# Three blocks of one model on one core: a mixer's tables and loads placed anew, and a written order from a mixer's end to the last mlp

## The chip, the core and the metric

The kernel runs on one core of one Trainium2 chip. A core has a matmul engine (TensorE, here PE, whose weight loads are shown apart as PEld), three elementwise engines (VectorE or DVE, ScalarE or ACT, GpSimd or POOL) and SyncE (SP), whose queue issues most loads. Each runs its own list of instructions in order and waits on semaphores where it needs what another has made. SBUF is the working memory of 128 partitions; matmuls write into PSUM, in banks of 128x512 f32 here. PE's granted clock is 2.4 or 1.2 GHz, shown as 1.0 or 0.5 of full speed.

The metric is the device time of one execution in microseconds (us). Before the change it is the median of three runs, 2019.61 us.

## The reference

For 512 positions of width 1024, in float32. One layer has a state-space mixer, the next an index-selected attention, each followed by a gated mlp; then a block of a hybrid attention with four kinds of heads, cross attention into 256 memory rows and an mlp; a norm ends it. The parts that the change touches:

```python
def s5_mixer(u, lam_re, lam_im, log_dt, b_re, b_im, c_re, c_im, d_skip, w_glu):
    lam = lax.complex(lam_re.astype(f32), lam_im.astype(f32))     # 64 groups x 64 states
    dt = jnp.exp(log_dt.astype(f32))[:, None]
    a_bar = jnp.exp(lam * dt)
    b_bar = ((a_bar - 1.0) / lam)[..., None] * lax.complex(b_re.astype(f32), b_im.astype(f32))
    bu = jnp.einsum('blgh,gph->blgp', ug, b_bar)
    _, states = lax.associative_scan(_ssm_combine, (a_seq, bu), axis=1)   # s_t = a_bar s_(t-1) + bu_t
    y = jnp.einsum('blgp,ghp->blgh', states, c).real.reshape(bsz, length, D_MODEL)
    y = jax.nn.gelu(y + d_skip.astype(f32) * u.astype(f32))
    val, gate = jnp.split(y @ w_glu, 2, axis=-1)
    return val * jax.nn.sigmoid(gate)

def second_block(...):
    x = x + hybrid_mixer(rmsnorm_2(x, g_mix[l]), w_in[l], g_group[l], sinks[l], w_out[l], rel_table)
    x = x + memory_cross_attention(rmsnorm_2(x, g_cross[l]), rmsnorm_2(mem, g_mem[l]),
                                   w_xq[l], w_xkv[l], w_xo[l])
    x = x + squared_relu_mlp(rmsnorm_2(x, g_mlp[l]), w_up[l], w_down[l])
    return rmsnorm_2(x, g_final)
```

## The kernel before

The stream x lies feature-major in eight tiles `x[0..7]` of 128 features x 512 positions. For a matmul every float32 operand is split into a high and a low part (`xH`, `xL`; `wH` by ACT at L127, `wL` by DVE at L128), and `mm3` (L33 to L35) does three matmuls per product: high by high, low by high, high by low. A 128x1024 piece of weight is loaded, split, and used by 128x512 matmuls into a PSUM bank. Behind a block's last projection DVE adds a bank to `x[d]` (L295), ACT makes `xH`, DVE `xL` (L274), and the squares for the next norm are added up (ACT squares, POOL adds, DVE the last, L287). PE then sums them over partitions (`st`, L258), DVE takes the inverse root in small steps, and PE spreads the result over partitions (`bcps`, L247).

**The state-space mixer** (`s5`, 0 to about 150 us) works in chunks of eight positions, in four quarters q of 16 groups. At the start three small loads (`lam`) give the real and imaginary eigenvalues and `log_dt`; PE lays them out (`par`, L1247), DVE takes exponentials and angles (`dt`, `er`), POOL builds the tables of rotations (`rt`, `rsum`), DVE the powers `pw` and `bw`; meanwhile ACT squares the input and PE transposes the scaled input (`ups`). Each quarter then goes through:

- input tables: three products (L1400, 128x1024, a power from `bw` times `bt`) and two sums (L1406, L1407) of them; output tables alike from `pw` and `cv`. DVE makes all 24 products; POOL makes the sums, except the first two, which DVE makes;
- `rotation`: five operations on 128x512 for cosines and sines (L1442 to L1446), the first quarter's on DVE, the others on POOL;
- PE: transposes of the tables (`btps`), contributions of the chunks (`vps`, two banks), a small convolution kernel (`kps`, copied by 8 DMAs into a zeroed tile `toep`), the outputs (`yps`, 64 matmuls a quarter, from `toep` and the states `W`);
- DVE: the states, 14 operations on `vps` banks (L1510 to L1523), two scans among them.

`in_order` (L85) makes DVE, POOL, ACT and PE each keep the written order within the mixer; elsewhere a scheduler decides, from what it thinks each instruction costs. The written order of the quarters is the loop `for q in range(5)` at the function's end. PSUM banks go round in three groups by a tag: 4 banks of "pj", 2 of "sc", 2 of "tp".

**The end of the hybrid mixer** (1567 to 1610 us): the norm of the last head group is spread (`bcps<-ident,norm`), the group scaled and split, and the last part of the output projection (`w_out`, rows 768 to 1023, `lin`, 48 matmuls) added to x. Beside it PE has the values of the cross attention (`mv`, 48 matmuls). Then `queries` projects x for the cross attention (`w_xq`, 48 matmuls, also called `lin` there), with the norm's factor applied to the result; `st` and `bcps<-ident,rs_y` make that factor. **The cross attention** (1610 to 1646 us) makes scores (`xs`), exponentials (L1110) and outputs, projects them (`xo`) onto x, and the last mlp begins.

Of the kernel before, what the change touches and what calls it, by code (L numbers as in the profile page):

```python
# [9 lines left out]
F32 = mybir.dt.float32  # L10
F32R = mybir.dt.float32r
I32 = mybir.dt.int32
AF = mybir.ActivationFunctionType
# [3 lines left out]
P = 128  # L17
S = 512
D = 1024
KT = D // P  # L20
NB = S // P
# [54 lines left out]
def ps(k, name, tag="tp"):  # L76
    return k.psum.tile([P, 512], F32, tag=tag, name=name, bufs={"pj": 4, "sc": 2, "tp": 2}[tag])


def tmp(k, name="t", dt=F32):  # L80
    return k.tmp.tile([P, 512], dt, tag="tmp", name=name)


@contextmanager
def in_order(k, *engines):  # L85

    traced = k.nc.cur_bb.bb.instructions
    last = traced[-1]
    yield
    start = next(i for i in reversed(range(len(traced))) if traced[i] is last) + 1  # L90
    for e in engines:
        mine = [i for i in traced[start:] if i.engine == e.engine]
        for first, second in zip(mine, mine[1:]):
            k.tc.add_manual_dep(second, first.name, mybir.DependencyInfo(mybir.DependencyClass.NoSync,
                                                                         mybir.DependencyReason.DATA), reason="in order")


WK = 4
# [3 lines left out]
CROSS_RATIO = 2.0  # L102
# [48 lines left out]
def linear_fm(*args):  # L151
    run(linear_steps(*args))
# [100 lines left out]
def norm_finish(k, bcast=True, tag="tp"):  # L253

    nc = k.nc
    st = ps(k, "st", tag)
    for i in range(NB):
        nc.tensor.matmul(st[:, i:i + 1], k.acc[:, i * P:(i + 1) * P], k.ones, start=True, stop=True)  # L258
# [33 lines left out]
def update_late(k, d, b, gain, last):  # L292


    k.nc.vector.tensor_add(k.x[d], k.x[d], b)  # L295
    after_update(k, d, gain if d < last else None)
    if d == KT - 1:
        for e in range(last, KT):
            emit_hl(k, e, gain)


def set_apart(pool, n):
# [145 lines left out]
def drive(main, side, ratio):  # L448


    due = 0.0
    for t in main:
        due += t * ratio
        while due > 0:
            t = next(side, None)
            if not t:
                due = 0.0
            else:
                due -= t
    for _ in side:  # L460
        pass
# [308 lines left out]
def hybrid(k, next_gain):  # L770
    nc, a = k.nc, k.a
    w = a["w_in_2"][0]
    k.p_bufs = HYB_DEPTH + 1
    with ExitStack() as es:
# [104 lines left out]
        def apply_norm(g):  # L879
            rb = bcast_tokens(k, norms[g], None)  # L880
            for j in (2 * g, 2 * g + 1):
                nc.vector.scalar_tensor_tensor(y[j], y[j], gg[:, j:j + 1], rb, op0=ALU.mult, op1=ALU.mult)
                split_hl(k, k.xH[j], k.xL[j], y[j])
# [113 lines left out]
            yield from pipelined([head(g, h) for g in cols for h in range(4)], HYB_DEPTH)  # L997

        drive(main(), side(), HYB_RATIO)
        run(cr.values())  # L1000
        apply_norm(3)
        linear_fm(k, wo, 6 * P, k.xH[6:], k.xL[6:], 0, D, lambda d, b: update_late(k, d, b, "cross", 6))
        cr.queries()
        drive(cr.main(lambda d, b: update_late(k, d, b, next_gain, 6)), cr.heads(), CROSS_RATIO)


class Cross:
# [68 lines left out]
    def queries(self):  # L1076
        k = self.k
        self.q = []

        def ev(m, b):  # L1080
            u = tmp(k, "xq")
            k.nc.vector.tensor_mul(u, b, normed(k))
            self.q += stack_q(k, self.fr, u)

        linear_fm(k, k.a["w_xq_2"][0], 0, k.xH, k.xL, 0, 256, ev)

    def heads(self):
        k = self.k
# [99 lines left out]
def s5(k, x, next_gain):  # L1188
    nc, a = k.nc, k.a
    G2 = 32  # L1190
    with ExitStack() as es:
# [11 lines left out]

        lam = ep.tile([64, 3, 64], F32, name="lam")
        for i, n in enumerate(("s5_lambda_re", "s5_lambda_im")):
            nc.sync.dma_start(lam[:, i], a[n][0])
        nc.sync.dma_start(lam[:, 2, 0:1], a["s5_log_dt"][0][:, None])
        braw = []
        for n in ("s5_b_re", "s5_b_im"):
            t_ = ep.tile([G2, 2, 64, 16], F32, name=n)  # L1210
# [148 lines left out]
        def b_steps():  # L1359
# [11 lines left out]
            yield nc.vector.tensor_add(bt[2], bt[0], bt[1])  # L1371
            yield nc.vector.tensor_sub(bt[1], bt[1], bt[0])

        norm = []
        interleave((norm.append(y) or y for y in rsqrt_steps(k, sb[:, :8], 1.0 / D, 8, tag="s5n")), b_steps())
        rs = norm[0]
        xs = ep.tile([P, G2, 8, 16], F32, name="xs")
        for j in range(8):
            o, i_ = xs[:, :, 7 - j], xt[j].rearrange("p (g h) -> p g h", h=16)
            if j % 2:  # L1380
                nc.vector.tensor_scalar(o, i_, rs[:, j:j + 1], None, op0=ALU.mult)
            else:
                nc.scalar.activation(o, i_, AF.Copy, scale=rs[:, j:j + 1])

        U = []
        for g in range(8):
# [7 lines left out]
        def products(q, names, w, n0, v):  # L1394

            gs = slice(q * 8, q * 8 + 8)
            out = []
            for n, (wi, vi) in zip(names, ((2, 0), (0, 1), (1, 2))):
                t_ = (big(n, 2) if n[0] == "Q" else wide(n)).rearrange("p (a b c) -> p a b c", a=8, b=8)
                nc.vector.tensor_mul(t_, w[:, n0:n0 + 8, wi, gs].rearrange("p t g -> p g t")[:, :, :, None].to_broadcast(sh4),  # L1400
                                     v[vi][:, gs, None, :].to_broadcast(sh4))
# [10 lines left out]
        st_ = [Ctx() for _ in range(4)]  # L1412

        def mid(name, bufs, pool=None):
            return (pool or qp).tile([P, 8, 64], F32, tag=name, name=name, bufs=bufs)
# [32 lines left out]
        def chunk(q):  # L1448
            s = st_[q]
            B = s.B  # L1450

            BT = []
            for ri in range(2):
                t_ = wide(("raw", "wH")[ri]).rearrange("p (a b) -> p a b", a=8)
                for hh in range(2):
                    b = ps(k, "btps", "tp")
                    for i in range(4):
                        nc.tensor.transpose(b[:, i * P:(i + 1) * P], B[ri][:, hh * 4 + i].rearrange("p t h -> p (t h)"), k.ident)
                    nc.scalar.activation(t_[:, hh * 4:hh * 4 + 4].rearrange("p a b -> p (a b)"), b, AF.Copy)
                BT.append(t_)  # L1460
            s.V = []
            for ri in range(2):
                b = ps(k, "vps", "pj")
                for i in range(8):
                    for t in range(2):
                        nc.tensor.matmul(b[t * 64:(t + 1) * 64, i * 64:(i + 1) * 64], BT[ri][:, i, t * 64:(t + 1) * 64],
                                         U[2 * q + i // 4][:, i % 4, t], start=True, stop=True)
                s.V.append(b.rearrange("p (i c) -> p i c", c=64))

        def constants_of(q):  # L1470

# [126 lines left out]
        for q in range(5):  # L1598
            if q < 3:
                input_tables(q + 1)  # L1600
            if q < 4:
                st_[q].Q = sums(st_[q].Q, nc.gpsimd)
            if q < 3:
                rotation(q + 1, nc.gpsimd)
            if q:
                outputs(q - 1)
            if q < 3:
                constants_of(q + 1)
                chunk(q + 1)
# [131 lines left out]
```

## Time and profile before

| what | value |
|---|---|
| median of three runs | 2019.61 us (2014.90 to 2022.14) |
| profiled execution | 2023.27 us, its span 2021.5 us |
| PE busy | 1895.9 us (94%), mean clock 0.967 |
| PEld busy | 1575.7 us (78%) |
| DVE busy | 1139.8 us (56%) |
| ACT busy | 823.9 us (41%) |
| POOL busy | 452.0 us (22%) |

The busy times are sums over the whole span; what a stage is bound by is read from that stage. In lists of waits an idle time is put down to the releaser that came last. A timeline row gives the start, the busy time and the number of equal instructions it stands for; in brackets how long the engine was idle before and what ended that. SPq is SP's queue. A clock of 0.50 in a stretch is 1.2 GHz.

### The profile page before, as it was taken

The page shows a single profiled execution, that of the slowest core. Times are in us where ns is not written, and L with a number is a line of the kernel's source. Part 1 is how long each engine was busy: PE and PEld are TensorE (multiplying, and loading weights), DVE is VectorE, ACT ScalarE, POOL GpSimd, SP SyncE. Part 2 cuts the span into 40 slices and gives each one's busy share as a digit, 9 for nine tenths or more (in the row PEclk, how much of TensorE's full clock was granted, in tenths as well). Part 3 has the DMA queues.
Part 4 walks back from the last instruction along what each step waited for, and adds up shares of the span by engine and source line. Part 5 has one row for each costly group of instructions (what it writes and reads, how often), then busy time and mean ns, then how long its engine had stood idle before and what let it go on. Part 6 is the DMA issues. An engine that isn't in the chain of part 4 may idle for free. (4 is left out here: it accounts for less than half of the span.)

```text
span 2021.5 us, 25029 instructions
## 1 busy us (share of the span) xinstructions
PE 1895.9 (94%) x9383; PEld 1575.7 (78%) x9383; DVE 1139.8 (56%) x2046; ACT 823.9 (41%) x1472; POOL 452.0 (22%) x468
## 2 busy tenths in 40 slices
PE   4899999999998878899999999999999779999997
PEld 3678888888887877778888888777787658888886
DVE  8953444334358987787443343567776674334343
ACT  3433332222234457666322222455564454233232
POOL 6840012001124655432120011212212120000001
PEclk9859999999999989999999999999999889999999
DMA  3113233333332322222333333333222213232332
GB/s 78 37 55 105 94 94 95 104 94 94 99 91 57 82 68 58 66 76 70 94 95 104 94 94 99 110 99 96 84 89 84 73 42 94 94 99 89 104 94 84
DMA packets 183939, 173.44 MB, mean 86 GB/s; under 512 B 11954, under 2 KB 178298, under 8 KB 183817
## 3 DMA queue, kind: packets, MB, share of 16 engines
q1 hardware_dynamic: 183048, 170.98, 28.3%
q8 instruction: 74, 1.21, 0.2%
q0 software_dynamic: 768, 0.86, 0.2%
q14 instruction: 49, 0.39, 0.1%
HBM read 158.92 MB, written 2.13 MB: 80 GB/s over the span
## 5 line engine op out<-in xcount | busy, mean ns | idle before, releaser
L128 DVE TENSOR_TENSOR wL<-raw,wH 128x1024 fp32r<-128x1024 f32 (+4 forms) x282 | 330.1, 1172 | 468.8 <-ACT wH L127 468.7
L127 ACT ACTIVATE wH<-raw 128x1024 fp32r<-128x1024 f32 (+4 forms) x314 | 308.4, 984 | 583.0 <-PE lin L34 432.4
L33 PE MATMUL lin<-xH,wH 128*128 128x512 f32 x1312 | 517.1, 395 | 6.1 <-ACT wH L127 2.4
L35 PE MATMUL lin<-xH,wL 128*128 128x512 f32 x1312 | 515.2, 393 | 5.2 <-DVE wL L128 5.2
L34 PE MATMUL lin<-xL,wH 128*128 128x512 f32 x1312 | 515.8, 393 | 0.0
L33 PEld LDWEIGHTS lin<-xH,wH 128*128 128x128 f32 x1312 | 248.3, 189 | 58.0 <-ACT wH L127 4.6
L35 PEld LDWEIGHTS lin<-xH,wL 128*128 128x128 f32 x1312 | 248.5, 189 | 57.5 <-DVE wL L128 6.9
L34 PEld LDWEIGHTS lin<-xL,wH 128*128 128x128 f32 x1312 | 248.6, 189 | 50.0 <-issue 0.5
L35 PE MATMUL lin<-hH,wL 128*128 128x512 f32 x608 | 236.7, 389 | 0.0
L33 PE MATMUL lin<-hH,wH 128*128 128x512 f32 x608 | 236.6, 389 | 0.0
L34 PE MATMUL lin<-hL,wH 128*128 128x512 f32 x608 | 236.5, 389 | 0.0
L287 POOL TENSOR_TENSOR acc<-acc,sq 128x512 f32<-128x512 f32 x42 | 64.5, 1535 | 593.1 <-ACT sq L286 592.1
L326 POOL TENSOR_TENSOR up<-up,ga 128x512 f32<-128x512 f32 x44 | 75.3, 1711 | 541.6 <-DVE up L325 541.6
L34 PEld LDWEIGHTS lin<-hL,wH 128*128 128x128 f32 x608 | 114.1, 188 | 23.7
L35 PEld LDWEIGHTS lin<-hH,wL 128*128 128x128 f32 x608 | 114.1, 188 | 23.7
L33 PEld LDWEIGHTS lin<-hH,wH 128*128 128x128 f32 x608 | 114.1, 188 | 23.6
L33 PE MATMUL qkv<-wH,xH 128*128 128x384 f32 x256 | 89.9, 352 | 6.8 <-ACT sqv L676 6.8
L34 PE MATMUL qkv<-wL,xH 128*128 128x384 f32 x256 | 89.6, 350 | 2.2 <-POOL wL L128 2.2
L35 PE MATMUL qkv<-wH,xL 128*128 128x384 f32 x256 | 89.6, 350 | 0.0
L179 ACT ACTIVATE hH<-up 128x512 fp32r<-128x512 f32 x44 | 27.9, 633 | 147.6 <-POOL up L326 147.6
L180 DVE TENSOR_TENSOR hL<-up,hH 128x512 fp32r<-128x512 f32 x44 | 30.5, 692 | 88.0 <-ACT hH L179 88.0
L422 POOL TENSOR_SCALAR p<-p,r 128x128 f32<-128x128 f32 (+1 forms) x96 | 55.1, 592 | 91.0 <-DVE r L420 50.6
(464 smaller groups left out, 2890.9 us busy)
## 6 DMA issues: line engine op xcount, KB each, us to landing
raw<-in_ffn_w_gate_up SPq DMA_DIRECT2D x88, 512.0 KB
raw<-in_ffn_w_down SPq DMA_DIRECT2D x40, 512.0 KB
raw<-in_w_up SPq DMA_DIRECT2D x32, 512.0 KB
raw<-in_w_down SPq DMA_DIRECT2D x28, 512.0 KB
raw<-in_dsa_w_in SPq DMA_DIRECT2D x96, 128.0 KB
raw<-in_w_in SPq DMA_DIRECT2D x20, 512.0 KB
raw<-in_s_w_glu SPq DMA_DIRECT2D x16, 512.0 KB
k<-k SPq DMA_DIRECT2D x30, 256.0 KB
```

The lines of the kernel that those rows point to most:

```text
L33: nc.tensor.matmul(out, wH, xH, start=start, stop=False)
L34: nc.tensor.matmul(out, wH, xL, start=False, stop=False)
L35: nc.tensor.matmul(out, wL, xH, start=False, stop=stop)
L127: nc.scalar.activation(wH, raw, AF.Copy)
L128: (l_engine or nc.vector).tensor_sub(wL, raw, wH.bitcast(F32))
L179: k.nc.scalar.activation(outH, src, AF.Copy)
L180: k.nc.vector.tensor_sub(outL, src, outH.bitcast(F32))
L287: (nc.vector if d == KT - 1 else nc.gpsimd).tensor_add(k.acc, k.acc, sq)
L326: nc.gpsimd.tensor_mul(u, u, acts[m])
L422: nc.gpsimd.tensor_scalar(p, p, r[:, b:b + 1], 1.0, op0=ALU.mult, op1=ALU.mult)
```

## The change

In the mixer: (1) the loads of the imaginary part and of `log_dt` are issued by ACT instead of SP; (2) the zeroing of `toep` and `cbd` moves from POOL's start behind its first rotation; (3) the first rotation moves from DVE to POOL; (4) ACT copies each quarter's powers (128x192 from `bw`, as many from `pw`) into one PSUM bank (`coef`), from which the products read; the second `vps` bank of quarters 1 to 3 is filled behind `kps`.

From the hybrid mixer's end on: (5) PE keeps the written order from the last norm's spreading through the queries, the output projection loads its weight in two pieces of 128x2x512, and the queries fill two banks with `st` between their parts; (6) in the cross attention's projection only the addition to x and the split follow a bank; the squares come after all eight and go into two sums, one by POOL and one by DVE, which `st` adds up in PSUM with eight matmuls.

```diff
-def in_order(k, *engines):
+def in_order(k, *engines, behind=False):
...
+        if behind:
+            mine.insert(0, next(i for i in reversed(traced[:start]) if i.engine == e.engine))
...
+    accs = k.acc if isinstance(k.acc, list) else [k.acc]
+    with in_order(k, nc.tensor, behind=len(accs) > 1):
+        for i in range(NB):
+            for j, acc in enumerate(accs):
+                nc.tensor.matmul(st[:, i:i + 1], acc[:, i * P:(i + 1) * P], k.ones, start=j == 0, stop=j == len(accs) - 1)
...
+def update_parts(k, d, b, gain, last):
+    k.nc.vector.tensor_add(k.x[d], k.x[d], b)
+    for e in [d] if d < last else range(last, KT) if d == KT - 1 else []:
+        emit_hl(k, e, gain)
+
+def norm_sums(k):
...
+    k.acc = [k.small.tile([P, S], F32, tag="acc", name="acc", bufs=1), tmp(k, "acc2")]
+    for d in range(KT):
+        e, acc = ((nc.gpsimd, nc.vector)[d // 4], k.acc[d // 4])
+        if d % 4 == 0:
+            nc.scalar.activation(acc, k.x[d], AF.Square)
+        else:
+            sq = tmp(k, "sq")
+            nc.scalar.activation(sq, k.x[d], AF.Square)
+            e.tensor_add(acc, acc, sq)
...
-        run(cr.values())
-        apply_norm(3)
-        linear_fm(k, wo, 6 * P, k.xH[6:], k.xL[6:], 0, D, lambda d, b: update_late(k, d, b, "cross", 6))
-        cr.queries()
-        drive(cr.main(lambda d, b: update_late(k, d, b, next_gain, 6)), cr.heads(), CROSS_RATIO)
+        with in_order(k, nc.tensor):
+            apply_norm(3)
+            run(cr.values())
+            for c in range(2):
+                wH, wL = load_w(k, wo, 6 * P, 2, [c * 512], 512)
+                for m in range(4):
...
+                    update_late(k, 4 * c + m, b, "cross", 6)
+            cr.queries()
+        drive(cr.main(lambda d, b: update_parts(k, d, b, next_gain, 6)), cr.heads(), CROSS_RATIO)
+        norm_sums(k)
...
+        banks = [ps(k, "xq", "pj") for _ in range(2)]
+        for k0 in range(0, KT, WK):
+            wH, wL = load_w(k, k.a["w_xq_2"][0], k0 * P, WK, [0], 256)
+            for m, b in enumerate(banks):
...
+                if k0 and m == 0:
+                    norm_finish(k, bcast=False)
+        k.rstd_b = bcast_tokens(k, k.rstd)
...
-            nc.sync.dma_start(lam[:, i], a[n][0])
-        nc.sync.dma_start(lam[:, 2, 0:1], a["s5_log_dt"][0][:, None])
+            (nc.sync, nc.scalar)[i].dma_start(lam[:, i], a[n][0])
+        nc.scalar.dma_start(lam[:, 2, 0:1], a["s5_log_dt"][0][:, None])
...
-        for t_ in toeps + cbds:
-            nc.gpsimd.memset(t_, 0.0)
...
+        def coefficients(q):
+            gs = slice(q * 8, q * 8 + 8)
+            s = st_[q]
+            b = ps(k, "coef", "pj" if q else "sc")[:, :384].rearrange("p (i n w g) -> p i n w g", i=2, n=8, w=3)
+            s.bw, s.pw = b[:, 0], b[:, 1]
+            yield nc.scalar.activation(s.bw, bw[:, :, :, gs], AF.Copy)
+            yield nc.scalar.activation(s.pw, pw[:, 1:, :, gs], AF.Copy)
...
-            st_[q].B = sums(products(q, ("raw", "wH", "wL"), bw, 0, bt), nc.gpsimd if q else nc.vector)
+            st_[q].B = sums(products(q, ("raw", "wH", "wL"), st_[q].bw, bt), nc.gpsimd if q else nc.vector)
...
-            st_[q].Q = products(q, ("wL", "Qi", "Qr"), pw, 1, cv)
+            st_[q].Q = products(q, ("wL", "Qi", "Qr"), st_[q].pw, cv)
...
+            s.BT, s.V = BT, []
+            contribution(q, 0)
...
-        rotation(0, nc.vector)
+        rotation(0, nc.gpsimd)
+        for t_ in cbds + toeps:
+            nc.gpsimd.memset(t_, 0.0)
...
         chunk(0)
+        contribution(0, 1)
+        run(coefficients(1))
...
+            if q < 2:
+                run(coefficients(q + 2))
...
                 kernel_of(q + 1)
+                contribution(q + 1, 1)
```

POOL's list at the mixer's start, before the change (`toep`, `cbd` and `W` are the zeroed tiles, `pw` the powers, `wH<-raw,wH` the first sum of products):

```order
L1217 DMA wL<-in_norm_mix 64x4x128 x2
L1239 MEMSET toep_92 128x2048
L1239 MEMSET toep_93 128x2048
L1239 MEMSET cbd_94 128x512
L1239 MEMSET cbd_95 128x512
...
L1338 TENSOR_TENSOR pw<-pw 128x8x32
L1590 MEMSET W_572 128x1024
...
L1406 TENSOR_TENSOR wH<-raw,wH 128x1024
```

And the same place with the change:

```order
L1262 DMA wL<-in_norm_mix 64x4x128 x2
...
L1380 TENSOR_TENSOR pw<-pw 128x8x32
L1496 TENSOR_TENSOR r_483<-rt,rsum 128x512
L1497 TENSOR_TENSOR sin<-rsum,rt 128x512
L1498 TENSOR_TENSOR cos<-rsum,rt 128x512
L1499 TENSOR_TENSOR cos<-r_483,cos 128x512
L1500 TENSOR_TENSOR sin<-r_483,sin 128x512
L1632 MEMSET cbd_94 128x512
...
L1632 MEMSET toep_93 128x2048
L1651 MEMSET W_578 128x1024
...
L1461 TENSOR_TENSOR wH<-raw,wH 128x1024
```

The zeros have left the start; between the table of powers and the first sum POOL now has five rotation operations and eight zeroings where it had four zeroings.

PE's list at the end of the hybrid mixer, before the change (`mv` the cross values, `norm` the last group's norm, `lin<-xH_1334` the output projection's last part, `lin<-xH_966` and the like the queries, `xs` the scores):

```order
L35 MATMUL wo<-xH_966,wL 128x512
L33 MATMUL mv<-wH,mHL_10623 128x256
...
L35 MATMUL mv<-wH,mHL_10630 128x256
L247 MATMUL bcps<-ident,norm_13084 128x128 x4
L33 MATMUL lin<-xH_1334,wH 128x512 x4
...
L35 MATMUL lin<-xH_1335,wL 128x512
L258 MATMUL st<-ones,acc 128x1 x4
L33 MATMUL lin<-xH_966,wH 128x512
...
L247 MATMUL bcps<-ident,rs_y 128x128 x4
L33 MATMUL lin<-xH_1275,wH 128x512
...
L207 MATMUL xs<-mk,q 128x256 x32
```

And with the change, where the queries are called `xq`:

```order
L35 MATMUL wo<-xH_961,wL 128x512
L250 MATMUL bcps<-ident,norm_13096 128x128 x4
L33 MATMUL mv<-wH,mHL_10635 128x256
...
L33 MATMUL lin<-xH_1346,wH 128x512
...
L33 MATMUL xq<-xH_961,wH 128x512
...
L264 MATMUL st<-ones,acc 128x1 x4
L33 MATMUL xq<-xH_1287,wH 128x512
...
L250 MATMUL bcps<-ident,rs_y 128x128 x4
L210 MATMUL xs<-mk,q 128x256 x32
```

The spreading of the last group's norm moves from behind the 48 `mv` matmuls to ahead of them, `st` from ahead of all queries to behind 36 of their 48 matmuls, and the second `bcps` behind all of them.

## Rows read from the trace of the kernel before

**Rows 1.** Mixer, busy us (instructions) of PE, PEld, DVE, ACT, POOL; clock, DMA.

```profile
34.20:126.30 92.10, 84.88 (x712) 69.03 (x712) 90.19 (x100) 43.16 (x97) 69.27 (x34) 0.79 0.13 39
126.30:148.65 22.35, 21.63 (x99) 15.17 (x97) 3.78 (x6) 6.88 (x12) 0.00 (x0) 0.50 0.16 49
74.00:76.00 2.00, 2.00 (x17) 1.44 (x16) 2.00 (x3) 0.00 (x0) 1.37 (x1) 1.00 0.00 0
92.00:94.00 2.00, 2.00 (x10) 1.34 (x9) 1.25 (x4) 0.92 (x3) 2.00 (x2) 0.50 0.00 0
```

**Rows 2.** The same view for the products of L1400 alone, DVE busy.

```profile
34.20:126.30 92.10, 41.42 (x24) 0.79 0.13 39
```

**Rows 3.** Timeline, PE in the mixer: start, us, operation, [idle before, releaser].

```profile
80.26 1.62 PE L1458 MATMUL btps<-ident,wL 128*128 128x128 f32 x8 [3.76 <-POOL wL L1407]
...
148.65 0.80 PE L33 MATMUL lin<-xH,wH 128*128 128x512 f32 x1
```

**Rows 4.** Busy times by stretch, end of the hybrid mixer.

```profile
1589.80:1595.10 5.30, 0.02 (x1) 0.00 (x0) 5.30 (x6) 5.25 (x8) 3.97 (x3) 0.78 0.13 47
1595.10:1603.20 8.10, 8.07 (x23) 6.66 (x24) 4.62 (x14) 0.00 (x0) 0.00 (x0) 0.51 0.40 125
1603.20:1608.00 4.80, 4.80 (x22) 3.94 (x21) 1.23 (x1) 1.06 (x1) 0.00 (x0) 1.00 0.02 8
```

**Rows 5.** Timeline, end of the hybrid mixer and start of the mlp.

```profile
1576.32 1.19 PE L33 MATMUL lin<-xH,wH 128*128 128x512 f32 x4 [2.22 <-ACT xH L179]
...
1584.03 0.50 PE L33 MATMUL lin<-xH,wH 128*128 128x512 f32 x1 [0.46 <-ACT wH L127]
...
1589.30 4.63 POOL L287 TENSOR_TENSOR acc<-acc,sq 128x512 f32<-128x512 f32 x3 [3.29 <-ACT sq L286]
...
1595.13 1.86 PE L258 MATMUL st<-ones,acc 128*128 128x1 f32 x8 [5.32 <-DVE acc L287]
...
1608.00 1.05 PE L247 MATMUL bcps<-ident,rs_y 128*128 128x128 f32 x8
...
1616.16 0.47 ACT L1110 ACTIVATE xp<-xs,nm 128x256 f32<-128x256 f32 x1 [1.60 <-DVE nm L1107]
...
1653.52 0.79 PE L35 MATMUL lin<-xH,wL 128*128 128x512 f32 x1 [4.43 <-DVE wL L128]
```

**Rows 6.** Timeline, the start.

```profile
0.74 1.28 ACT L1276 ACT_TABLE_LOAD   x1 [0.74 <-PEq L1729]
...
2.42 0.60 SPq L1207 DMA_DIRECT2D lam<-in_s_log_dt  x1
...
3.23 0.42 PE L1247 MATMUL par<-ident,lam 64*64 64x32 f32 x4 [3.23 <-DMA lam<-in_s_lambda_re]
...
5.21 3.57 POOL L1239 MEMSET toep<- 128x2048 f32 x2
...
6.89 0.43 PE L1247 MATMUL par<-ident,lam 64*64 64x32 f32 x4 [0.95 <-DMA lam<-in_s_log_dt]
...
7.66 2.08 DVE L1173 TENSOR_SCALAR dt_x<-par 128x32 f32<-128x32 f32 x1
...
9.78 0.27 DVE L1174 TENSOR_SCALAR dt_k<-dt_x 128x32 f32<-128x32 f32 x1
```

**Rows 7.** Timeline, rotation 0 on DVE, later ones on POOL, and one step of the states.

```profile
40.45 1.08 DVE L1442 TENSOR_TENSOR r<-rt,rsum 128x512 f32<-128x512 f32 x1
...
44.14 0.68 DVE L1446 TENSOR_TENSOR sin<-r,sin 128x512 f32<-128x512 f32 x1
...
64.20 2.45 POOL L1443 TENSOR_TENSOR sin<-rsum,rt 128x512 f32<-128x512 f32 x1
...
78.00 0.68 DVE L1514 TENSOR_TENSOR vps<-vi,vps 128x512 f32<-128x512 f32 x1
...
93.25 1.27 POOL L1446 TENSOR_TENSOR sin<-r,sin 128x512 f32<-128x512 f32 x1
```

**Rows 8.** Durations of L1400: count, ns least/median/most, first and last start.

```profile
L1400 DVE TENSOR_TENSOR Qr<-pw,cv x4: 1218/2474/2483, 49.0 to 112.0; 128x1024 f32<-128x1024 f32 x4
```

More of the change, by code (lines that the diff above doesn't have):

```diff
@@ L256, in norm_finish @@
     st = ps(k, "st", tag)
-    for i in range(NB):
-        nc.tensor.matmul(st[:, i:i + 1], k.acc[:, i * P:(i + 1) * P], k.ones, start=True, stop=True)
+    accs = k.acc if isinstance(k.acc, list) else [k.acc]
[3 more added lines that the diff above has]
+                nc.tensor.matmul(st[:, i:i + 1], acc[:, i * P:(i + 1) * P], k.ones, start=j == 0, stop=j == len(accs) - 1)
     k.rstd = rsqrt_small(k, st[:, :NB], 1.0 / D, NB, tag="nrm")
@@ L299, in update_late @@
             emit_hl(k, e, gain)
+def update_parts(k, d, b, gain, last):
[3 more added lines that the diff above has]
+def norm_sums(k):
+    nc = k.nc
+    k.rstd = k.rstd_b = None
+    k.acc = [k.small.tile([P, S], F32, tag="acc", name="acc", bufs=1), tmp(k, "acc2")]
[7 more added lines that the diff above has]
+            e.tensor_add(acc, acc, sq)
 def set_apart(pool, n):
@@ L999, in hybrid @@
         drive(main(), side(), HYB_RATIO)
-        run(cr.values())
-        apply_norm(3)
-        linear_fm(k, wo, 6 * P, k.xH[6:], k.xL[6:], 0, D, lambda d, b: update_late(k, d, b, "cross", 6))
-        cr.queries()
-        drive(cr.main(lambda d, b: update_late(k, d, b, next_gain, 6)), cr.heads(), CROSS_RATIO)
+        with in_order(k, nc.tensor):
[4 more added lines that the diff above has]
+                for m in range(4):
+                    b = ps(k, "lin", "pj")
+                    cs = slice(m * P, (m + 1) * P)
+                    for i in range(2):
+                        mm3(nc, b, wH[:, i, cs], wL[:, i, cs], k.xH[6 + i], k.xL[6 + i], i == 0, i == 1)
+                    update_late(k, 4 * c + m, b, "cross", 6)
+            cr.queries()
+        drive(cr.main(lambda d, b: update_parts(k, d, b, next_gain, 6)), cr.heads(), CROSS_RATIO)
+        norm_sums(k)
 class Cross:
@@ L1078, in queries @@
         self.q = []
-        def ev(m, b):
+        banks = [ps(k, "xq", "pj") for _ in range(2)]
+        for k0 in range(0, KT, WK):
+            wH, wL = load_w(k, k.a["w_xq_2"][0], k0 * P, WK, [0], 256)
+            for m, b in enumerate(banks):
+                c = slice(m * P, (m + 1) * P)
+                for i in range(WK):
+                    mm3(k.nc, b, wH[:, i, c], wL[:, i, c], k.xH[k0 + i], k.xL[k0 + i], k0 + i == 0, k0 + i == KT - 1)
+                if k0 and m == 0:
+                    norm_finish(k, bcast=False)
+        k.rstd_b = bcast_tokens(k, k.rstd)
+        for b in banks:
             u = tmp(k, "xq")
-            k.nc.vector.tensor_mul(u, b, normed(k))
+            k.nc.vector.tensor_mul(u, b, k.rstd_b)
             self.q += stack_q(k, self.fr, u)
-        linear_fm(k, k.a["w_xq_2"][0], 0, k.xH, k.xL, 0, 256, ev)
     def heads(self):
@@ L1372, in b_steps @@
             yield nc.vector.tensor_sub(bt[1], bt[1], bt[0])
+        def coefficients(q):
[5 more added lines that the diff above has]
+            yield nc.scalar.activation(s.pw, pw[:, 1:, :, gs], AF.Copy)
+        st_ = [Ctx() for _ in range(4)]
         norm = []
@@ L1376, in s5 @@
         rs = norm[0]
+        first = coefficients(0)
+        next(first)
         xs = ep.tile([P, G2, 8, 16], F32, name="xs")
@@ L1383, in s5 @@
                 nc.scalar.activation(o, i_, AF.Copy, scale=rs[:, j:j + 1])
+        run(first)
         U = []
@@ L1392, in s5, with products @@
             U.append(t_.rearrange("p (i t c) -> p i t c", i=4, t=2))
-        def products(q, names, w, n0, v):
+        def products(q, names, w, v):
             gs = slice(q * 8, q * 8 + 8)
@@ L1399, in products @@
                 t_ = (big(n, 2) if n[0] == "Q" else wide(n)).rearrange("p (a b c) -> p a b c", a=8, b=8)
-                nc.vector.tensor_mul(t_, w[:, n0:n0 + 8, wi, gs].rearrange("p t g -> p g t")[:, :, :, None].to_broadcast(sh4),
+                nc.vector.tensor_mul(t_, w[:, :, wi].rearrange("p t g -> p g t")[:, :, :, None].to_broadcast(sh4),
                                      v[vi][:, gs, None, :].to_broadcast(sh4))
@@ L1411, in s5 @@
         sh3 = [P, 8, 8, 8]
-        st_ = [Ctx() for _ in range(4)]
         def mid(name, bufs, pool=None):
@@ L1460, in chunk, with contribution @@
                 BT.append(t_)
[L1461 to L1468, printed above, removed]
+            s.BT, s.V = BT, []
+            contribution(q, 0)
+        def contribution(q, ri):
+            s = st_[q]
+            b = ps(k, "vps", "pj")
+            for i in range(8):
+                for t in range(2):
+                    nc.tensor.matmul(b[t * 64:(t + 1) * 64, i * 64:(i + 1) * 64], s.BT[ri][:, i, t * 64:(t + 1) * 64],
+                                     U[2 * q + i // 4][:, i % 4, t], start=True, stop=True)
+            s.V.append(b.rearrange("p (i c) -> p i c", c=64))
         def constants_of(q):
```

## The prediction

> **What bounds the kernel now.** PE, the matmul engine, leads the busy times of the page by far, so only a stretch where PE waits, or runs at its lower clock, can give time back. To find such stretches I read what each engine waited for in the two places that the change touches, then those places as busy times by stretch, and last as single instructions. The reader is to see two different pictures.
>
> In the state-space mixer (0 to 148.65 us, where the gated projection begins [rows 3]) VectorE (DVE) is the busiest: 90.19 of 92.10 us between 34.2 and 126.3 us, 41.42 of them in the 24 products of L1400 [rows 1, 2]. But it decides only at two places. At the start PE has no work until DVE has scaled the input. In the middle it waits for GpSimd (POOL), which sums the products: 3.76 us before the third quarter's transposes [rows 3]. Behind that PE works nearly without a gap, mostly at its 1.2 GHz level: in 2 us it finishes 10 matmuls there, against 17 at 2.4 GHz, and from 126.3 to 148.65 us it is busy 21.63 of 22.35 us at 0.50 of full clock [rows 1].
>
> At the end of the hybrid mixer the waits are the bound: 2.22 us before the last part of the output projection, 5.32 us before the sums `st` of the norm, with almost no matmul for 5.3 us, and then a stretch of 8.1 us at 0.51 of full clock [rows 4, 5]. Where the last mlp begins PE waits another 4.43 us for a weight's low part [rows 5].
>
> **The state-space part, step by step.** *Loads on two queues.* `log_dt` is issued at 2.42 us, as the last of three on SP; its matmuls run at 6.89 us, those of the first load at 3.23 [rows 6]. ScalarE (ACT) has nothing to do until 0.74 us; with one load of 0.6 us ahead of it, `log_dt` is issued there at about 1.35, 1.1 us earlier, and that is the lower end. At most it lands with the first load: 6.89 - 3.23 = 3.66. I take 2.3, the middle. [...]
>
> *Zeros later.* The first small DVE step, `dt_x`, takes 2.08 us beside the zeroing of `toep`; the next one, of the same shape, takes 0.27 [rows 6]. Without the zeros there 1.8 us go; bounds 0, if it was something else that slowed it, and 1.8. The zeros, 3.57 us for `toep` and less for `cbd`, now stand on POOL behind its first rotation and ahead of its first sums.
>
> *Rotation 0 on POOL.* DVE loses five operations, 40.45 to 44.8 us, 4.3 us in all [rows 7]. POOL takes them directly after its table of powers, so they run beside DVE's sums of quarter 0, two additions of a product's size. A product takes 1.22 us alone and up to 2.48 [rows 8]; I price both additions at the dear end, +2.3, bounds 0 and 2.5. POOL's own price is 1.27 to 2.45 an operation [rows 7]: five are 6.4 to 12.3 us, with the zeros 10 to 16 behind the table, about when its first sums come due.
>
> *Powers in PSUM.* The slow products run beside POOL with both operands in SBUF: of the `Qr` ones the median is 2.47 us, the least 1.22 [rows 8]. With one operand in PSUM the row to go by is `vps<-vi,vps` at 78.00 us: 0.68 us for half the elements while POOL is busy [rows 7]. So I take 24 x 1.22 = 29.3 us instead of 41.4; DVE is 12 us earlier at the end. Bounds: nothing gained, and 2 x 0.68 = 1.36 a product, 8.8 gained. [...] ACT gets two copies a quarter. PE now also waits for DVE before the first `xps`, and before one half of each `vps`, since banks are used again; behind that half stands `yps`. DVE should be ahead by then, so I price this at 0, and at 3 us if it is not.
>
> *Sum.* DVE's chain at the front is 2.3 + 1.8 = 4.1 us earlier, and the first sums 4.1 - 2.3 = 1.8. The first transposes need the sums and PE's own chain, which follows the 4.1: between the two, 2.7. POOL's second sums, behind faster products, then come so much earlier that the 3.76 us go too: 2.7 + 3.76 = 6.4 us. After that PE has no wait of size left to lose. **State-space part: -6.4 us**; bounds with an unchanged clock +1 (front gains nothing, a bank costs 3, half of the wait goes) and -10 (3.66 + 1.8 + 3.76, rounded up for the small waits).
>
> **The hybrid end.** The broadcast `bcps` of the last head group now goes ahead of the 48 `mv` matmuls, so scaling and splitting lie beside these: the 2.22 goes. Weight stalls before `lin` (one of three such is 0.46 [rows 5]) go with two wider weight loads in place of four: 1 us. In the fixed order 36 `xq` matmuls go ahead of `st`, in two banks; at 22 in 4.8 us [rows 4] they are 7.9 us, and the sums on POOL (4.63 us for three [rows 5]) lie beside them. I don't count the whole 5.32 as won, since `xq` itself waits for DVE, which has an addition, a split and parts of the weights to do per block: 2 us of waiting stay, 3.3 go. Without the long idle the clock should stay up; 8.1 us at 0.51 are work of 4.1, so 4 go. From 2.2 + 1 + 3.3 + 4 = 10.5 nothing is taken off for the chain from broadcast to scores, 8.16 us from 1608.00 to the first exponential at 1616.16 [rows 5]: it had matmuls beside it and now has none, but they did not hold it. **-10.5 us**, bounds -4 (the waits only move to `xq`) and -12.5. At the mlp start the additions and splits no longer have the squares' additions between them, and the first weight's split comes earlier: of the 4.43 us I take 2, bounds 0 and 3.5. The sums come later there, but the norm is first needed behind blocks of matmuls. **Hybrid end: -12.5 us.**
>
> Total 6.4 + 12.5 = 18.9. The profiled execution took 2023.27 us, 1.8 outside its span, 3.66 above the median of 2019.61; 2023.27 - 18.9 - 3.66 gives **2000.7 us** for the median.
>
> **The rivals.** *Clock (B).* If PE, with fewer waits, gets back to 2.4 GHz in one to three of the last `yps` passes, each of 64 matmuls falls from 12.8 to 7.5 us (at 10 and 17 in 2 us [rows 1]). For: the first pass reached full clock. Against: the later ones did not, and they had no idle time before them either. It gives 5 to 16 more: 1985 to 1995.
>
> *Only the hybrid end (C).* In the mixer PE is held by something else: by POOL with a rotation at 2.45 an operation and the zeros ahead of its sums, or by a coefficient bank. Then -12.5 alone: 2007.
>
> *Only the mixer (D).* The fixed order blocks: `xq` stands in front of `st` and waits for DVE, whose splits are slow beside POOL; PE's idle time only moves, and the clock falls as before. Then -6.4, at most a few more: 2009 to 2013.
>
> *Slower (E).* Products from PSUM, with a strided and repeated operand, cost d each instead of 1.22. DVE's work without them up to 126.3 is 126.3 - 41.4 - 4.1 - 4.3 = 76.5, and PE needs 22.35 more: the mixer would end at 98.9 + 24 d. It eats what the hybrid end gives from d = (148.65 + 12.5 - 98.9) / 24 = 2.6 us on; at d = 3.2 the time is 2034. The 0.68 of [rows 7], for half the elements, speaks against it.
>
> **How the numbers follow.** Forecast 0.52, its own range 1995 to 2006; B 0.20; C 0.13; D 0.10; E 0.04; the rest 0.01. What this kernel's measurement can tell from no change is 0.3%, 6 us, so faster means under 2013.6. The forecast, B, C and most of D would be faster, 0.92 in all; the runs of before alone lie 7 us apart, which can blur D, so 0.87. Same 0.09, slower 0.04. The range from 1987 to 2012 leaves out the lower part of B, a little of D, and E.
>
> **What would show it.** In the changed profile: `dt_x` near 0.3 us and `log_dt`'s matmuls between 3.2 and 5.8; all 24 products near 1.2, none at 2.4; no wait of PE for POOL's `wL` over 1 us; the gated projection at about 142 us; no wait of 5 us before `st` and the clock near 1 there; the first exponential 10 us earlier against `mv`; under 3 us of waiting for the mlp's first low part. The work between 150 and 1560 us should only move. Wrong would be: the gated projection at 148 or later, products over 1.4, PE waiting for DVE before `xps` or `vps`, or a new wait of several us before `xq`.

## The result and the profile after

The changed kernel took 1993.97 us in the median of four runs (1990.43 to 1997.47) against 2018.89 for the kernel before in the same comparison: ratio 0.9887, 95% interval [0.9861, 0.9913]. On four other chips the kernel before had medians of 2012.3 to 2013.5 us; on one of them the changed kernel was timed again, 1992.78, ratio 0.9914 [0.9881, 0.9947]. So the gain is about 1%, 17 to 25 us; I had forecast 18.9. The measured 1993.97 lies just under the forecast's own range (1995 to 2006) and inside rival B's (1985 to 1995).

The page of the changed kernel, head and busy times:

```profile
span 1991.1 us, 25027 instructions
...
PE 1876.7 (94%) x9391; PEld 1564.7 (79%) x9391; DVE 1118.3 (56%) x2041; ACT 827.2 (42%) x1478; POOL 447.2 (22%) x470
```

The two profiled executions lie 30.4 us apart in span, more than the medians: before's was one of its longer ones. The traces show PE's granted clock as 1.0 or 0.5 of full speed; the 2.4 and 1.2 GHz of the texts on record are names for these two levels, and no run measured a frequency. Executions of one program differ by how long PE runs at 0.5, so the mean granted clock that each run lists is read with its time. Over 80 runs of the kernel before (2007 to 2025 us, mean clock 0.962 to 0.976, on average 0.9715) time falls by 1.37 us for each 0.001 of clock, with 2.1 us of scatter about that line. "At equal clock" below is a kernel's mean distance from this line, "by clock" the rest. The line is drawn through before's runs and goes a little past them for kernels at 0.978. It takes a lower clock to cost the same wherever in the program it occurs, which no run tests.

**The start**, answering to [rows 6, 7]: a timeline of the changed kernel.

```profile
1.32 0.61 ACTq L1252 DMA_DIRECT2D lam<-in_s_log_dt  x1
...
3.27 0.94 PE L1289 MATMUL par<-ident,lam 64*64 64x32 f32 x12 [3.27 <-DMA lam<-in_s_lambda_re]
...
4.55 0.18 DVE L1218 TENSOR_SCALAR dt_x<-par 128x32 f32<-128x32 f32 x1
...
30.00 1.45 POOL L1496 TENSOR_TENSOR r<-rt,rsum 128x512 f32<-128x512 f32 x1
...
35.30 2.28 DVE L1462 TENSOR_TENSOR wL<-raw,wL 128x1024 f32<-128x1024 f32 x1
...
37.64 1.09 PE L1512 MATMUL btps<-ident,wL 128*128 128x128 f32 x8 [1.69 <-DVE wL L1462]
```

All twelve `par` matmuls run at once at 3.27 us: the third load lands with the first. `dt_x` takes 0.18 us instead of 2.08. DVE's sums are slower beside POOL's rotation (1.54 and 2.28 us, 1.21 each before), though by less than priced, and the first transposes start at 37.64 instead of 41.41.

**The products**, answering to [rows 8]: durations of their line, ns least, median, most.

```profile
L1455 DVE TENSOR_TENSOR raw<-coef,bt x4: 1215/1221/1224, 30.4 to 85.2; 128x1024 f32<-128x1024 f32 x4
...
L1455 DVE TENSOR_TENSOR Qr<-coef,cv x4: 1216/1217/1220, 42.9 to 100.2; 128x1024 f32<-128x1024 f32 x4
```

No product takes more than 1.23 us with its power read from PSUM. The fastest `Qr` product before, with both operands in SBUF, took 1.22 [rows 8], so a read from PSUM costs nothing that shows.

**The end of the hybrid mixer**, answering to [rows 5]: a timeline.

```profile
1547.16 1.05 PE L250 MATMUL bcps<-ident,norm 128*128 128x128 f32 x8
...
1566.82 0.50 PE L35 MATMUL xq<-xH,wL 128*128 128x512 f32 x1 [1.56 <-DVE wL L131]
...
1575.05 0.95 PE L264 MATMUL st<-ones,acc 128*128 128x1 f32 x8
...
1578.71 1.05 PE L250 MATMUL bcps<-ident,rs_y 128*128 128x128 f32 x8
...
1587.23 0.47 ACT L1155 ACTIVATE xp<-xs,nm 128x256 f32<-128x256 f32 x1 [3.01 <-DVE nm L1152]
...
1622.96 0.50 PE L35 MATMUL lin<-xH,wL 128*128 128x512 f32 x1 [3.74 <-DVE wL L131]
```

The reader is to see that PE has almost no idle time any more ahead of `st`: the one wait that the view lists there is 1.56 us, in `xq`. From the spreading of the last norm to the first exponential it is 40.1 us. Before, the same stretch began with `mv` and took 48.9:

```profile
1567.28 0.29 PE L33 MATMUL mv<-wH,mHL 128*128 128x256 f32 x1
```

**The clock in the four `yps` passes**, busy us and granted clock (third number from the end) for each: first the kernel before, then the changed one.

```profile
66.90:80.20 13.30, 9.59 (x66) 6.66 (x65) 13.30 (x12) 3.97 (x8) 12.06 (x6) 0.87 0.15 44
91.20:105.40 14.20, 14.20 (x65) 9.79 (x65) 13.30 (x19) 1.96 (x5) 11.71 (x6) 0.50 0.26 78
117.80:132.40 14.60, 13.92 (x66) 9.41 (x65) 8.46 (x13) 1.62 (x4) 3.62 (x2) 0.51 0.15 44
134.20:148.60 14.40, 14.38 (x65) 9.70 (x64) 3.78 (x6) 4.49 (x8) 0.00 (x0) 0.50 0.25 74
```

The same view of the changed kernel, in the same columns, with its own times for the four passes:

```profile
64.60:73.90 9.30, 9.30 (x66) 6.65 (x64) 9.30 (x15) 0.60 (x1) 9.30 (x5) 0.85 0.21 62
85.50:94.60 9.10, 9.10 (x66) 6.53 (x64) 9.10 (x12) 0.60 (x1) 7.01 (x4) 0.87 0.34 102
106.30:116.10 9.80, 9.10 (x68) 6.40 (x65) 9.50 (x14) 1.24 (x3) 2.05 (x1) 0.89 0.23 67
117.40:129.40 12.00, 11.22 (x64) 7.67 (x64) 3.78 (x6) 5.08 (x9) 0.00 (x0) 0.72 0.30 89
```

The last three passes have the same 64 matmuls, 43 us at 0.5 before and 31 us at 0.72 to 0.89 after. The gated projection begins at 129.42 us instead of 148.65, where I had put it at 142. Before's profiled execution was one of its longer ones, so these 19 us are more than the change brings: in `hyb_only` below, whose mixer is before's, the projection begins at 144.87.

### The profile page after: what moved, and what is told of

Same layout as the page of the kernel before. It is cut to its first block, busy times and chain, and to the rows that moved or that the text cites. A ratio compares the mean times of both kernels' runs of the same rounds, so it can differ in the third digit from the quotient of the medians.

```text
span 1991.1 us, 25027 instructions
## 1 busy us (share of the span) xinstructions
PE 1876.7 (94%) x9391; PEld 1564.7 (79%) x9391; DVE 1118.3 (56%) x2041; ACT 827.2 (42%) x1478; POOL 447.2 (22%) x470
## 3 DMA queue, kind: packets, MB, share of 16 engines
q8 instruction: 74, 1.21, 0.2%
## 5 line engine op out<-in xcount | busy, mean ns | idle before, releaser
L35 PE MATMUL lin<-xH,wL 128*128 128x512 f32 x1296 | 507.6, 392 | 4.0 <-DVE wL L131 4.0
L33 PE MATMUL lin<-xH,wH 128*128 128x512 f32 x1296 | 508.6, 393 | 1.6 <-ACT wH L130 1.6
L34 PE MATMUL lin<-xL,wH 128*128 128x512 f32 x1296 | 507.7, 392 | 0.0
L35 PEld LDWEIGHTS lin<-xH,wL 128*128 128x128 f32 x1296 | 244.2, 188 | 54.6 <-DVE wL L131 4.8
L33 PEld LDWEIGHTS lin<-xH,wH 128*128 128x128 f32 x1296 | 244.2, 189 | 50.9 <-ACT wH L130 2.1
L34 PEld LDWEIGHTS lin<-xL,wH 128*128 128x128 f32 x1296 | 244.4, 189 | 49.3 <-issue 0.5
L293 POOL TENSOR_TENSOR acc<-acc,sq 128x512 f32<-128x512 f32 x36 | 56.3, 1565 | 568.0 <-ACT sq L292 567.3
L182 ACT ACTIVATE hH<-up 128x512 fp32r<-128x512 f32 x44 | 27.9, 633 | 147.6 <-POOL up L354 147.6
```

What stands on the lines that cost most here:

```text
L33: nc.tensor.matmul(out, wH, xH, start=start, stop=False)
L34: nc.tensor.matmul(out, wH, xL, start=False, stop=False)
L35: nc.tensor.matmul(out, wL, xH, start=False, stop=stop)
L182: k.nc.scalar.activation(outH, src, AF.Copy)
L293: (nc.vector if d == KT - 1 else nc.gpsimd).tensor_add(k.acc, k.acc, sq)
```

## The experiments

All were timed against the kernel before. In the table the interval is that of the ratio; the last two columns are the split explained above, with 95% bounds from the scatter and the line.

| kernel | what it is | median, runs | ratio | mean clock | at equal clock | by clock |
|---|---|---|---|---|---|---|
| changed, both times | all of it | 1993.6, 10 | 0.9887; 0.9914 | 0.977 | -10.6 ± 1.7 | -7.6 |
| s5_only | mixer part | 1999.94, 6 | 0.9931 [0.9915, 0.9947] | 0.978 | -4.0 ± 2.1 | -9.1 |
| hyb_only | hybrid's end | 2007.15, 12 | 0.9963 [0.9944, 0.9981] | 0.972 | -6.2 ± 1.3 | -0.4 |
| front_only | loads, zeros, rotation | 2014.89, 10 | 1.0006 [0.9988, 1.0023] | 0.971 | +0.4 ± 1.4 | +0.4 |
| psum_only | powers, late vps | 2008.52, 10 | 0.9982 [0.9963, 1.0] | 0.975 | 0.0 ± 1.5 | -4.6 |
| vps_late | late vps alone | 2013.55, 12 | 1.0001 [0.9985, 1.0016] | 0.974 | +2.8 ± 1.4 | -3.4 |
| vps_early | mixer part without it | 2010.0, 12 | 0.998 [0.9961, 0.9999] | 0.971 | -4.7 ± 1.3 | +0.9 |
| yt_late | yt behind kps instead | 2011.84, 12 | 0.9988 [0.9973, 1.0004] | 0.973 | -0.7 ± 1.3 | -1.6 |
| both_late | changed, all of vps late | 2001.17, 6 | 0.9923 [0.9896, 0.995] | 0.977 | -7.4 ± 2.1 | -8.0 |
| upd_old | changed, old updates | 1998.63, 6 | 0.992 [0.9892, 0.9949] | 0.976 | -9.1 ± 2.0 | -6.6 |
| cbd_early | changed, cbd moved | 1992.49, 5 | 0.9894 [0.9873, 0.9916] | 0.978 | -12.3 ± 2.2 | -8.6 |
| cbd_all | the same, quarter 1's still earlier | 1989.8, 6 | 0.9878 [0.9852, 0.9904] | 0.979 | -14.6 ± 2.2 | -9.5 |

**The two halves apart.** `s5_only` has the changed function `s5` in the kernel before, `hyb_only` the reverse.

> The kernel before with the whole mixer part of the change, and the hybrid mixer's end as before. Theory: the mixer gave about 20 of the 30 us by which the two profiled executions differ, 6.4 of it waits of PE that are gone and some 13 its clock, which now comes back to 2.4 GHz in each of the yps passes. So the gated projection begins at 128 to 131 us, and the time is 17 to 21 us under before. Rival: the clock came back by chance in one execution; then the projection begins near 142, and the time is 6 to 8 us under before.

> The kernel before with the written order from the hybrid mixer's end to the mlp, and the state-space mixer as before. Theory: worth 9.7 us, as the offsets of the two traces say (8.7 by the first exponential, 1.0 behind it), so 8 to 11 us under before. Rival: a part of it only came because the mixer ahead was changed (other state of the clock, loads earlier); then 4 to 7 us.

The mixer part gives 13.5 us, between theory and rival: 4.0 at equal clock and 9.1 by clock. Five of its six runs have a mean clock of 0.977 or more, which no run of before has, so the clock's return is no accident of one execution. The profiled one is the sixth, at 0.974, and its gated projection begins at 133.79 us. The hybrid's end gives 6.3, which is the rival's figure, and its clock is before's. But the rival's reason doesn't show: at equal clock the halves give 4.0 and 6.2 and the whole 10.6, so no part shows that needs both halves. The theory's 9.7 was read from one pair of executions.

**The mixer's edits apart.** `front_only`:

```diff
-        rotation(0, nc.vector)
+        rotation(0, nc.gpsimd)
+        for t_ in cbds + toeps:
+            nc.gpsimd.memset(t_, 0.0)
```

(with the two loads on ACT), and `psum_only` the rest of the mixer part.

> The kernel before with three of the mixer's edits: two loads on ACT's queue, the zeros later, rotation 0 on POOL. Products still read SBUF. Theory: PE is 2 to 4 us ahead up to yps of quarter 0, but POOL's sums of quarter 2 still wait for slow products, so the wait of 3 to 4 us before the third quarter's transposes stays, and the yps passes stay at 1.2 GHz; the gated projection begins at 144 to 147, the time is 2 to 5 us under before. Rival: the early start alone brings the clock back, then 131 to 136 and 12 to 17 us.

> The kernel before with the mixer's other edit alone: the powers in PSUM, which also puts one half of vps behind kps. Loads, zeros and rotation 0 as before. Theory: all products take 1.22 us, the 3.76 us before the third quarter's transposes go, and the clock comes back in the yps passes, since the tables arrive early; the gated projection begins at 130 to 134, the time is 14 to 18 us under before. Rival: only the wait goes and the clock stays at 1.2 GHz; then 144 to 146 and 3 to 5 us.

`front_only` misses both: the front alone is worth nothing. PE's first long wait ends 3.6 us earlier, but the first transposes then wait 5.0 us for DVE's sums beside POOL, by the list of waits, and start at 41.85 us. The time of `psum_only` lies in its rival's range (3 to 5 us), but not for the rival's reason: the powers alone bring half of the clock and nothing at equal clock. POOL's wait is gone from its list, and in its place PE waits 5.0 us for ACT's copies of the transposes, where it was 1.3 before. The gated projection begins at 139.95 and 137.38 us, in neither of the ranges expected.

**Where the clock comes from.** The powers' edit also moved half of `vps` behind `kps`. `vps_late` makes that move alone, `vps_early` takes it alone out of the mixer part:

```diff
             s.BT, s.V = BT, []
             contribution(q, 0)
+            contribution(q, 1)
...
                 kernel_of(q + 1)
-                contribution(q + 1, 1)
```

> The kernel before with one edit alone: the second half of vps of quarters 1 to 3 goes behind kps, as in the change; products read SBUF, front as before. In all traces so far PE's clock falls 3 to 5 us after each kps begins; what differs is how long it stays at 1.2 GHz. Theory A: that vps half, dense work right ahead of yps, is what lets the clock rise again. Then the mean clock is 0.975 to 0.978 instead of 0.9715 and the time 5 to 9 us under before. Theory B: it is the tables and waits (products from PSUM). Then the clock stays at 0.971 to 0.973 and the time within 3 us of before.

> The whole mixer part, with one edit taken back: both halves of vps ahead of kps, as before the change; hybrid end as before. Theory A (the vps half brings the clock back): the mean clock falls from 0.978 to 0.971 to 0.974 and of the 13 us of the mixer part 3 to 6 are left. Theory B (tables and waits do): the clock stays at 0.977 to 0.979 and the time at 1999 to 2003.

This is the clearest pair, though the two were timed on different chips. Between `s5_only` and `vps_early` only that place differs; at equal clock they are the same (-4.0 and -4.7), but the clock is 0.978 against 0.971, and 10 us go with it. None of the twelve runs of `vps_early` is above 0.976. The passes of `vps_early` in the view used above:

```profile
66.50:79.20 12.70, 12.70 (x66) 8.80 (x65) 11.83 (x17) 2.26 (x3) 12.62 (x8) 0.58 0.15 46
90.10:101.10 11.00, 11.00 (x67) 7.64 (x66) 10.95 (x15) 1.00 (x3) 8.09 (x4) 0.69 0.33 101
112.50:126.80 14.30, 13.60 (x66) 9.36 (x66) 8.65 (x13) 1.68 (x4) 1.29 (x1) 0.56 0.15 44
127.90:137.00 9.10, 8.29 (x64) 5.83 (x64) 3.78 (x6) 5.12 (x9) 0.00 (x0) 1.00 0.36 111
```

Alone on the kernel before (`vps_late`) the move raises the clock less, from 0.9715 to 0.974, between the ranges of the two theories, and costs 2.8 us at equal clock, so that nothing is left. In its list of waits a new one stands ahead of the last `yps` pass, with no releaser shown:

```profile
PE yps L1543 <- issue: 4.1, 1, 4.1
```

So theory A is borne out by `vps_early`, and by `vps_late` only in part.

`yt_late` asks whether any dense work at that place does it: in `vps_early` the transposes `yt` go behind `kps`.

> The kernel vps_early (whole mixer part, both halves of vps ahead of kps, clock 0.971) with the transposes yt of the quarter before moved from ahead of kps to behind it, so that other dense PE work than vps stands between kps and yps for quarters 2 and 3. Theory A: any such work lets the clock rise in the yps passes: mean clock 0.974 to 0.978, 4 to 9 us less than vps_early (2010). Theory B: it is something about vps itself (its wait for DVE, or when the states start): the clock stays at 0.969 to 0.973, the time at 2007 to 2013.

The clock rises by 0.002 only, and the time is no better, since at equal clock the move costs 4.0 us: the general form of theory A is not borne out. Two of the four passes get `yt`, though, where three get `vps`, so it isn't excluded. `both_late` moves the other half of `vps` too.

> The changed kernel with both halves of vps of quarters 1 to 3 behind kps. Theory A: still more dense work between kps and yps, the clock rises at least as early (mean 0.978 to 0.982), 0 to 4 us less than the changed kernel. Theory B: no change of the clock; DVE's states of a quarter begin 4 us later, which its slack covers or which costs 1 to 4 us a quarter: 0 to 8 us more.

The clock stays where it was and the time at equal clock rises by 3.2 ± 2.2 us: theory B. Of the two, moving one half is better.

**The mlp's start.** `upd_old` takes back `update_parts` and `norm_sums`.

> The changed kernel with one edit taken back: squares and sums of the last norm again follow each block of the cross attention's projection, in one sum. Theory: between the first exponential and the spreading of that norm the traces with and without this edit take about the same time (49.6 to 51.2 against 48.9 to 51.6 us), so it is worth 0 to 1 us: the time within 2 us of the changed kernel's 0.9887 of before. Rival: the 2 us that I forecast; then 0.9895 to 0.990.

At equal clock 1.5 us more, with bounds that hold 0 and the rival's 2: not settled. In its trace PE's waits there are 4.42 and two of 1.5 in all, against the 3.74 above, so a wait does shrink by 2.2.

**Where the mixer's 6.4 us went.** PE's waits before the transposes from 29 to 130 us (us in total, times, longest), first in the kernel before:

```profile
PE btps L1458 <- POOL wL L1407: 5.1, 2, 3.8
PE btps L1458 <- ACT raw L1459: 1.3, 3, 0.6
```

and in the changed kernel:

```profile
PE btps L1512 <- ACT raw L1513: 4.8, 4, 1.6
...
PE btps L1512 <- DVE wL L1462: 1.7, 1, 1.7
```

A timeline of ACT and PE in the same kernel, at the third quarter's transposes:

```profile
74.06 0.60 ACT L1602 ACTIVATE y<-yps 128x512 f32<-128x512 f32 x1 [3.45 <-PE yps L1601]
...
74.56 1.25 ACT L1533 ACTIVATE cbd<-cv 64x128 f32<-64x128 f32 x4
...
75.83 1.08 ACT L1513 ACTIVATE raw<-btps 128x512 f32<-128x512 f32 x2
...
76.48 1.14 PE L1512 MATMUL btps<-ident,wH 128*128 128x128 f32 x8 [1.45 <-ACT raw L1513]
```

No wait for POOL's `wL` is left. But ACT stands between: it makes `y`, then `cbd`, then the copy that PE waits for. In the kernel before, PE waited 1.3 us in all for these copies, since they lay beside its wait for POOL. The sum of the waits is the same, 6.4 us before and 6.5 after; what the mixer gains at equal clock is about the earlier start. `cbd_early` writes `cbd` ahead:

```diff
+            if q < 3:
+                constants_of(q + 1)
             if q:
                 outputs(q - 1)
             if q < 3:
-                constants_of(q + 1)
                 chunk(q + 1)
```

> The changed kernel once more, to be compared with the next two on one chip and to have more than four runs of it. Theory: mean clock 0.977 to 0.980, time 18 to 23 us under before (0.9887 to 0.991).

> The changed kernel with ACT's four cbd copies (1.25 us a quarter) written ahead of the outputs of the quarter before instead of between them and the copies of the transposes. Theory: the mixer gained only 3 us at equal clock, not 6.4, because behind POOL's wait a wait for ACT stood: PE waits 1.45 us before the second half of the transposes of quarters 2 and 3, since ACT does y (0.6) and cbd (1.25) first. Then these two waits fall to 0.2 to 0.4 us and the time is 2 to 3 us under the changed kernel's at the same mean clock. Rival: ACT is not what holds, the transposes then wait for PSUM banks or y; the waits stay over 1 us and the time at equal clock within 1 us.

The changed kernel's second set has a mean clock of 0.976 and a gain of 17 us by the ratio, both just short of what was expected: in two of its six runs the clock is 0.969 and 0.972, at before's level, and the time 2009 and 2006 us.

In `cbd_early` the wait for ACT falls from 4.8 to 2.4 us in all, and at equal clock the kernel is 1.7 ± 2.3 us ahead of the changed one: the wait is shown, its price is not settled by this run. `cbd_all` does it for quarter 1 too.

```diff
         decay(0)
+        constants_of(1)
         kernel_of(0)
...
+            if q in (1, 2):
+                constants_of(q + 1)
             if q:
                 outputs(q - 1)
```

> The kernel cbd_early with quarter 1's cbd copies written ahead of the first kps too, where ACT waited 4 us for kps, so that the last of PE's waits for ACT before the second half of the transposes (1.6 us, quarter 1) goes. Theory: no such wait over 0.4 us is left, and at equal clock the time is 1 to 2 us under cbd_early and 2.5 to 4 us under the changed kernel; the median 1988 to 1993. Rival: at quarter 1 POOL's sums come last, and the 1.6 us turn into a wait for them; then within 0.5 us of cbd_early at equal clock.

PE's waits in `cbd_all`, in the same stretch and columns (us in total, times, longest):

```profile
PE btps L1512 <- DVE wL L1462: 1.6, 1, 1.6
PE btps L1512 <- ACT raw L1513: 1.1, 4, 0.4
```

No such wait over 0.4 us is left, and the time at equal clock is 4.0 ± 2.2 us under the changed kernel's and 2.3 ± 2.5 under `cbd_early`'s. Its median of 1989.8 us is the lowest of all, below both kernels; its interval still overlaps that of the changed kernel.

## Why the prediction was right, and where not

The time and the sign were right, 24.9 us against 18.9. But the sum is not made as I said: both terms were too large, and the clock, my rival B, came on top and filled the gap. At equal clock the change gives 10.6 us, so that the number came out near is in good part luck: two errors of opposite sign.

- *Loads.* 3.6 us, my upper end; I took 2.3. `log_dt` is issued 1.1 us earlier and its matmuls run 3.6 earlier; whether the queue or the other loads ahead of it held it, no run separated.
- *Zeros.* 1.9 us on `dt_x`, as forecast (1.8).
- *Rotation 0.* DVE's two sums take 3.8 us instead of 2.4, +1.4 where I put 2.3 (the dear end of my rows was 2.5). POOL is done with it 8.7 us after it starts. In the changed kernel the first transposes are 3.8 us earlier (forecast 2.7), in the other traces with the mixer part 2.4 to 3.8.
- *Powers in PSUM.* Right for the products: 12 us of DVE are gained as taken, though the bounds beside that term, 0 and 8.8, left it out. The step that failed is "I price this at 0, and at 3 us if it is not" for the half of `vps` behind `kps`: I looked only at its wait. PE did not wait there, and the place raised the clock of the passes behind it, worth 10 us between `s5_only` and `vps_early`. I had B at 0.20 without a lever that would bring it about.
- *The sum of the mixer.* "After that PE has no wait of size left to lose" was wrong. I let a wait of 3.76 us go without asking what was late next; it was ACT, 4.8 us in all instead of 1.3. The part measured -4.0 ± 2.1 instead of -6.4, and `cbd_all` gets 4.0 ± 2.2 us by removing that wait.
- *The hybrid's end.* Sized at 12.5, measured 6.2 ± 1.3 at equal clock. `hyb_only` alone in a timeline, its spreading of the last norm, first and last exponential, and the mlp's wait and norm:

```profile
1559.16 1.05 PE L250 MATMUL bcps<-ident,norm 128*128 128x128 f32 x8
...
1599.25 0.47 ACT L1155 ACTIVATE xp<-xs,nm 128x256 f32<-128x256 f32 x1 [3.01 <-DVE nm L1152]
...
1604.30 1.09 ACT L182 ACTIVATE pt<-ptps 128x512 fp32r<-128x512 f32 x2 [1.29 <-PE ptps L415]
...
1609.03 0.24 ACT L1155 ACTIVATION_READ_ACCUMULATOR xp<-xs,nm 128x1 f32 x1
...
1636.82 0.80 PE L35 MATMUL lin<-xH,wL 128*128 128x512 f32 x1 [4.81 <-DVE wL L131]
...
1650.89 1.13 PE L250 MATMUL bcps<-ident,rs_y 128*128 128x128 f32 x8 [0.16 <-DVE rs_y L218]
```

  The same places in the kernel before, and the last of its query matmuls with what follows them:

```profile
1608.81 0.48 PE L33 MATMUL lin<-xH,wH 128*128 128x512 f32 x1
...
1611.85 2.18 PE L207 MATMUL xs<-mk,q 128*128 128x256 f32 x16
...
1620.56 1.08 ACT L179 ACTIVATE pt<-ptps 128x512 fp32r<-128x512 f32 x2
...
1666.08 1.13 PE L247 MATMUL bcps<-ident,rs_y 128*128 128x128 f32 x8 [0.17 <-DVE rs_y L215]
```

  To the first exponential it is 40.1 us against 48.9: -8.8 where I had -10.5. The waits ahead of `st` went as forecast or better, from 8.7 us in all to 1.6 (I had 6.5 of gain), and the clock is 1.00 from the spreading of the last norm to the second `bcps`. `st` itself comes no earlier, 27.9 us after the start of the stretch in both; the gain is that 36 of the query's matmuls lie ahead of it. What failed is "nothing is taken off for the chain from broadcast to scores". Before, the last twelve query matmuls ran behind the second `bcps`, 3.0 us beside that chain. Now they stand ahead of it, between `st` and `bcps`, where they take 2.9 us (1575.86 to 1578.71 in the changed kernel), and the chain itself is no shorter, 8.5 us against 8.16.

  From the first exponential to the spreading of the mlp's norm I had -2. In this trace it is 51.6 us against 49.9 before (1616.16 to 1666.08), in the two traces of the changed kernel 48.9 and 49.5: between -1.0 and +1.7, so no gain is shown there. PE's wait where the mlp begins is still 3.74 us in the changed kernel, and I had put it under 3. The sixteen exponentials take 9.8 us in this trace from the first to the last reading of a sum, 8.9 before (1616.16 to 1625.03). The copies of the first transposed probabilities (`pt`) stand between them on ACT in both; here ACT is idle for 1.29 us ahead of these copies, waiting for PE's transposes, where before the change it went straight on to them. That this is the cause was read from the traces and not tried.
- *The rivals.* B happened, beside the sum and not in place of it. C and D did not happen as such: each half counts. E is excluded at 1.22 us a product.

## What to carry to other kernels

Before counting a wait as won, follow the waiting instruction's other inputs and see which comes next: here a 3.76 us wait hid an engine that was about 1.5 us late in three of the quarters, and moving some of that engine's work into its idle time got 4 us. Where a stretch of matmuls runs at either clock level from one execution to the next, list the mean clock with every time and compare kernels at equal clock; without that, two profiles had me expect 20 us of the mixer part, where 13.5 came. And a written order sets more than waits: the same instructions in another place moved the clock by 0.007 and the time by 10 us.

## What the runs showed of the hardware

In most of the mixer's `kps` series, nearly all of whose matmuls are 128x32, PE's granted clock falls to 0.5 of full speed 2 to 5 us after the series begins. In the kernel before it falls 3.9 to 4.6 us after each of the four starts (46.05, 62.67, 86.84 and 113.6 us) and comes back after 3.4 us in the first two quarters, after 20.5 in the third and, in the last, not until the gated projection (34 us). The same program differs in this between executions: behind the last series of the changed kernel the clock is back after 3.4 us in one trace (there it falls again at 118.6 us) and after 13.8 in the other (`after_again`). It isn't so after each `kps`: in the third quarter of `upd_old` the series begins at 84.87 us and the clock stays at 1.0 until the next series, to 108.0; in that of `cbd_all` it begins at 76.92 and the clock stays at 1.0 to 99.75. The place of one half of `vps` between `kps` and `yps` changes how soon it comes back on average: the mean clock is 0.978 with it there (`s5_only`) and 0.971 without (`vps_early`). Why is open: a `yps` pass has the same 64 matmuls in both cases, and other dense work (`yt`) at that place brought 0.973.
